# Cosine-similarity attention: the first pair split by head, ten K scales moved to VectorE, and instruction orders read from a table

## The chip, the cores and the metric

One core of a Trainium2 chip runs the whole kernel. A core has a matrix engine (TensorE, PE in the profile), three engines for elementwise work (VectorE or DVE, ScalarE or ACT, GpSimd or POOL), and SyncE (SP), which here only issues transfers between the chip's memory (HBM) and the core's memory (SBUF). PE writes to a second memory, PSUM, which is divided into banks. Each engine runs its own list of instructions in the order of the program and waits on semaphores for the others. The metric is the time of one execution in microseconds; the time before is the median of 8 runs, 197.62 us (196.11 to 199.24).

## The reference

```python
def reference(Q, K, V, tau):                       # each 8 x 12 x 512 x 64, float32; tau = 0.1
    Q_norm = Q / (np.linalg.norm(Q, axis=-1, keepdims=True) + 1e-10)
    K_norm = K / (np.linalg.norm(K, axis=-1, keepdims=True) + 1e-10)
    scores = np.einsum('bhqd,bhkd->bhqk', Q_norm, K_norm) / tau
    weights = np.exp(scores - np.max(scores, axis=-1, keepdims=True))
    weights = weights / (np.sum(weights, axis=-1, keepdims=True) + 1e-10)
    return np.einsum('bhqk,bhkd->bhqd', weights, V).astype(np.float32)
```

There are 96 heads of 512 queries and 512 keys with 64 numbers each. Every row of Q and K is divided by its length, so that a score lies between -10 and 10, and the maximum need not be subtracted.

## The kernel before

The kernel works on **48 pairs** of heads. For each pair these operations are made (the names are the keys in the code, and stand in the prediction as words):

- LD (L289) and LV (L292) load Q, K and V of the pair, 256 KB each, on SP. ST (L462) stores the result. Eighteen pairs of Q and K can lie in SBUF at once, and six of V.
- SQ squares Q and K. For most pairs this is one instruction on POOL over 1,024 numbers in each of 128 partitions (L310). For pairs 0, 1 and 2 the table `SQ_ON` gives Q and K separately to ACT, DVE or POOL (L303, L305).
- RED sums the squares of each row: on DVE directly (L335), or in two steps, SSQ on PE (L324), which adds eight groups of columns, and a shorter reduction on DVE (L331). One sum of every later pair, and both sums of pairs 1 to 3, go by PE.
- NEW makes one over the root of the sums. For pairs 0, 1 and 2 it is a logarithm and an exponential on ACT (LOG, L348, and L350) and a copy of Q's half to PSUM on DVE (L353). From pair 3 on it is made for two pairs at once, in eight short steps on DVE (L355 to L364).
- SCL multiplies with it and writes bf16 (L382): Q on DVE, **K on POOL** for all pairs. The list `K_ON_DVE`, which would send K to DVE, is empty.
- TR transposes on PE (L388, four instructions each for Q and K), and EVA copies the result from PSUM to SBUF: one copy on DVE (L405); for pair 0 K's half on ACT (L396) and Q's half on DVE (L400).
- SCO makes the scores on PE (L413). A pair has four chunks `c` of 128 keys, each for both heads. EXP takes the exponential of one chunk of both heads, 1,024 columns, on ACT (L424), straight from two PSUM banks. There are two such places, so the scores of chunk `c` wait for the exponential of chunk `c - 2`.
- VC converts V to bf16 on POOL (L429), with a column of ones beside it, so that PV, the product of the weights with V on PE (L438), also gives the sum of the weights. RCP (L453) and NRM (L455) on DVE divide by it.

Twelve matmuls on zeros (`warm`, L247) run on PE while the first loads are on their way.

**What sets the order.** Every operation is added to one list with a due time (`START`, `PERIOD` and the rest) and the operations that it needs. `schedule` plays them through with a table of durations, `TIMES`, and so fixes the order of each engine's instructions. Between due times 16.0 and 180.5 PE and ACT keep strictly to the order of the due times, as SP does throughout; DVE and POOL take what can start first among the next 60. `run` then writes each engine's list with the waits that are left. The order is thus fixed in the program; on the chip an engine stands at an instruction until its operands are there, whatever is ready behind it. SP loads in the order Q, K of pairs 0, 1, 2, then V of pair 0, and then Q, K and V in turn. POOL begins with the square of Q1, the K scales of pairs 0 and 1, V0, and the squares of pairs 3 and 4. ACT begins with the square of Q0, the square of K1, pair 0's logarithm, both squares of pair 2, and pairs 1's and 2's roots, all ahead of the first exponential.

Of the kernel before, what the change touches and what calls it, by code (L numbers as in the profile page):

```python
# [3 lines left out]
ALU = mybir.AluOpType  # L4
# [13 lines left out]
class Program:  # L18

    TIMES = {
        "exp": (0.903, 1.055), "exp1": (0.477, 0.63), "sqa": (0.48, 0.63), "sm_act": (0.12, 0.26),
        "cpa": (0.48, 0.63), "table": (1.3, 1.3),
        "sco": (0.322, 0.39), "pv": (0.127, 0.31), "tr": (0.223, 0.39), "warm": (4.4, 4.5),
        "eva": (0.597, 0.69), "eva1": (0.33, 0.42), "nrm": (0.34, 0.425), "rcp": (0.09, 0.178), "sclq": (0.593, 0.677),
        "red": (0.6, 0.685), "new": (0.11, 0.2), "sqv": (0.6, 0.69), "sm_dve": (0.1, 0.2),
        "sq": (1.85, 1.9), "sqp": (0.97, 1.02), "sclk": (1.0, 1.045), "vc": (0.585, 0.63), "sm_pool": (0.3, 0.35),
        "ld": (0.05, 2.1), "ssq": (0.245, 0.41), "redp": (0.131, 0.23),
    }  # L30
    WIRE = 0.72
    LATENCY = {"pe": 0.056, "act": 0.042, "dve": 0.038, "pool": 0.08, "sp": 0.08}
    SWITCH = 0.09
    START = {"sp": 0.8, "pool": 0.7, "dve": 0.7, "pe": 0.7, "act": 0.8}
    HEAD, TAIL = 16.0, 180.5
    FIXED = ("sp", "pe", "act")

# [10 lines left out]
    def schedule(self):  # L48
        engines = ("sp", "pool", "dve", "pe", "act")
        pending = {e: sorted((o for o in self.list if o.eng == e), key=lambda o: o.due) for e in engines}  # L50
        order = {e: [] for e in engines}
        free = dict(self.START)
        wire = 1.0
        tiled = False

        def ready_at(o):
            t = 0.0
            for n in o.needs:
                p = self.ops[n]
                if p.end is None:  # L60
                    return None
                if p.eng != o.eng or o.eng in ("dve", "pool") or o.own:
                    t = max(t, p.end + self.LATENCY[o.eng])
            return t

        left = len(self.list)
        while left:
            best = None
            for e in engines:
                pick = None  # L70
                wide = 1 if e == "sp" or e in self.FIXED and pending[e] and self.HEAD < pending[e][0].due < self.TAIL else 60
                for o in pending[e][:wide]:
                    r = ready_at(o)
                    if r is None:
                        continue
                    start = max(r, free[e])
                    if pick is None or start < pick[0] - 1e-9:
                        pick = (start, o)
                if pick is not None and (best is None or pick[0] < best[0]):
                    best = pick  # L80
            assert best is not None, [
                (e, [(o.key, [n for n in o.needs if self.ops[n].end is None]) for o in pending[e][:4]]) for e in engines]
            start, o = best
            e = o.eng
            pending[e].remove(o)
            order[e].append(o)
            left -= 1
            pitch, dur = self.TIMES[o.kind]
            if e == "pe":
                if o.kind == "sco" and not tiled:  # L90
                    start = max(start, free[e] + self.SWITCH)
                tiled = o.kind == "sco"
            o.start = start
            if o.slot is not None:
                wire = max(wire, start) + self.WIRE
                o.end = wire + dur
                free[e] = start + pitch
            else:
                o.end, free[e] = start + dur, start + pitch
        self.model_us = max(o.end for o in self.list)  # L100
        return order
# [67 lines left out]
def bass_cosine_similarity_attention_kernel(  # L169
# [71 lines left out]
    P.add("table", "act", "table", -1000, [], lambda e: e.preload_act_table_set("natural_log_exp_and_others"))  # L241
# [7 lines left out]

    P.add("wz", "dve", "sm_dve", -100, [], lambda e: e.memset(warm_in[:, :], 0.0))  # L250
# [28 lines left out]

    def pair(s):  # L280
# [6 lines left out]
        for w, x in ((0, Q), (1, K)):  # L287
            P.add(("LD", s, w), "sp", "ld", s, [key("SCL", s - R_QK, w), key("SQ", s - R_QK, 0)],
                  lambda e, w=w, x=x: e.dma_start(out=qk[iq][:, w], in_=src(x, s)),  # L289
                  slot=f"first{s}_{w}" if s in SQ_ON else f"qk{iq}")  # L290
# [5 lines left out]
        red = [key("RED", s - R_SQ, 0), key("RED", s - R_SQ, 1)]  # L296
        if s in SQ_ON:
            for w, eng in enumerate(SQ_ON[s]):
# [5 lines left out]
                else:  # L304
                    emit = lambda e, half=half, dst=dst: e.tensor_tensor(out=dst, in0=half, in1=half, op=ALU.mult)  # L305
                P.add(("SQ", s, w), eng, {"act": "sqa", "dve": "sqv", "pool": "sqp"}[eng],
                      due_sq(s) + 0.1 * w, [("LD", s, w), red[w]], emit)
        else:
            P.add(("SQ", s, 0), "pool", "sq", due_sq(s), [("LD", s, 0), ("LD", s, 1)] + red,
                  lambda e: e.tensor_tensor(out=sqf, in0=data, in1=data, op=ALU.mult))  # L310

        m = 8 * sizes[g]
# [3 lines left out]
        for w in range(2):  # L316
            sqs = ("SQ", s, w if s in SQ_ON else 0)
            dst = x2[:, w, c8 : c8 + 8]
            if (s, w) in session:
# [10 lines left out]
                P.add(("RED", s, w), "dve", "redp", due + 0.1, [("SSQ", s, w), key("NEW", g - R_X, 7)],  # L330
                      lambda e, bank=bank, dst=dst: e.tensor_reduce(  # L331
                          out=dst, in_=o_ps[bank][:, 320:384].rearrange("p (g e) -> p g e", e=8), axis=AX.X, op=ALU.add))
            else:
                P.add(("RED", s, w), "dve", "red", due_red(s) + 0.5 * w, [sqs, key("NEW", g - R_X, 7)],
# [5 lines left out]
        rq_g, rk_g = n_ps[:, g % R_X, 128 : 128 + m], xs[g][:, m : 2 * m] if acts else rk[g % R_X][:, 0:m]  # L340
        on_dve = [i for i in range(first[g], first[g] + sizes[g]) if i in K_ON_DVE]
        free = [[("SCL", i, k) for i in range(first[g - R_X], first[g - R_X] + sizes[g - R_X])] if g >= R_X else []
                for k in range(2)]
        reds = [("RED", i, w) for i in range(first[g], first[g] + sizes[g]) for w in range(2)]
        if s == first[g] and g in NORM_ON_ACT:
            at = NORM_ON_ACT[g]
            P.add(("LOG", g), "act", "sm_act", at, reds + ["eps"],
# [4 lines left out]
            P.add(("NEW", g, 6), "dve", "new", TF - 2.6, [("NEW", g, 7)],  # L352
                  lambda e: e.tensor_copy(out=rq_g, in_=xs[g][:, 0:m]))  # L353
# [22 lines left out]
        for w in range(2):  # L376
            dve = w == 0 or s in K_ON_DVE
            r = (tg[:, m + c8 : m + c8 + 8] if dve else rk_g[:, c8 : c8 + 8]) if w else rq_g[:, c8 : c8 + 8]
            r = r.rearrange("p (h t) -> p h t", h=2).unsqueeze(3).to_broadcast([128, 2, NT, DIM])
            P.add(("SCL", s, w), "dve" if dve else "pool", "sclq" if dve else "sclk", T0 - (2.85 if w and not dve else 2.55) - slack(s, M_SCL),  # L380
                  [("NEW", g, 6 + w + (dve and w)), key("TR", s - R_QN, w)],
# [4 lines left out]
            def tr(e, w=w):  # L386
                for t in range(NT):
                    last = e.transpose(  # L388
                        (t_k0 if s == 0 and w else t_ps[:, w])[:, t, :], qn[iqn][:, w, t].rearrange("p h d -> p (h d)"), ident[:, :])
                return last  # L390

            P.add(("TR", s, w), "pe", "tr", T0 - PERIOD + 0.9 * TR_AT[w],
                  [("SCL", s, w), key("EVA", s - 1) if not (s == 1 and w) else ("EVA", 0), "eye"], tr)
        if s == 0:
            P.add(("EVA", s, 1), "act", "cpa", -50, [("TR", s, 1)],
                  lambda e: e.activation(  # L396
                      out=qt[iqt][:, 1].rearrange("p t x -> p (t x)"),
                      in_=t_k0.rearrange("p t x -> p (t x)"), func=ACT.Copy))
            P.add(("EVA", s), "dve", "eva1", -50, [("TR", s, 0)],
                  lambda e: e.tensor_copy(  # L400
                      out=qt[iqt][:, 0].rearrange("p t x -> p (t x)"),
                      in_=t_ps[:, 0].rearrange("p t x -> p (t x)")))
        else:
            P.add(("EVA", s), "dve", "eva", T0 - 1.5, [("TR", s, 0), ("TR", s, 1), key("SCO", s - R_QT, NT - 1)],
                  lambda e: e.tensor_copy(  # L405
                      out=qt[iqt][:, :, :, :].rearrange("p w t x -> p (w t x)"),
                      in_=t_ps[:, :, :, :].rearrange("p w t x -> p (w t x)")))
        for c in range(NT):
            b = c % 2

            def sco(e, c=c, b=b):
                for h in range(2):
                    last = e.matmul(  # L413
                        out=sc_ps[:, 2 * b + h, :], lhsT=qt[iqt][64 * h : 64 * h + 64, 1, c, :],
                        rhs=qt[iqt][64 * h : 64 * h + 64, 0, :, :], start=True, stop=True)
                return last

            P.add(("SCO", s, c), "pe", "sco", T0 + 0.9 * c,
                  [("EVA", s), ("EVA", s, 1) if s == 0 else None, ("EXP", s, c - 2) if c >= 2 else key("EXP", s - 1, c + 2)], sco)
            for h in range(2) if last_pair and c == NT - 1 else (None,):  # L420
                hs = slice(0, 2) if h is None else slice(h, h + 1)
                P.add(("EXP", s, c) if h is None else ("EXP", s, c, h), "act", "exp" if h is None else "exp1", T0 + 0.9 * c + (h or 0) * 0.1,
                      [("SCO", s, c), key("PV", s - R_ET, 1, NT - 1)],
                      lambda e, c=c, b=b, hs=hs: e.activation(  # L424
# [54 lines left out]
WARM = 12  # L479
# [11 lines left out]
def slack(s, most):  # L491
    return most * min(1.0, s / 12)
# [33 lines left out]
```

## Time and profile before

| | |
|---|---|
| median of 8 runs | 197.62 us (196.11 to 199.24) |
| the profiled execution | 197.44 us, of which the span from its first to its last instruction is 195.5 us |
| ACT busy | 182.8 us, 93% of the span |
| PE busy | 177.6 us, 91% (the ends of matmuls are modelled) |
| DVE busy | 164.6 us, 84% |
| POOL busy | 162.8 us, 83% |
| first exponential starts | 11.16 us |
| the 193 exponentials | 177.4 us busy, 1,152 ns mean of one |
| mean granted PE clock | 0.991 |

A row of a timeline gives the start and the length in us, then the engine, the line of the kernel, the operation, what is written from what, the shapes, and how many instructions are merged (x). In brackets stands the idle time of the engine before it, and what ended the wait. Instructions of one engine overlap a little, so the time from one start to the next is shorter than the length of one. A row of the windows gives one stretch of time and how long each engine was busy in it.

### The profile page before, as it was taken

Reading aid. Unit: us, or ns where it says so; the run is one execution under the profiler, and the core shown is the slowest. Engines: PE = TensorE matmul, PEld = TensorE weight load, DVE = VectorE, ACT = ScalarE, POOL = GpSimd, SP = SyncE. Lnnn points to the kernel's source line nnn. Section 1 sums busy time; section 2 is a strip of 40 time slices with the busy share of each in tenths; the row PEclk is TensorE's granted clock in tenths of the full one; section 3 lists DMA queues with packets and bytes.
Section 4 is the critical chain, followed back from the end, with each engine's and each line's share of the span. In section 5 each row is a group of like instructions: output and inputs, shape, how many; then the busy total and the mean of one; then the engine's idle time right before and its main releaser. Section 6 shows DMA issues by size and latency. Waiting matters only on the chain.

```text
span 195.5 us, 6712 instructions
## 1 busy us (share of the span) xinstructions
PE 177.6 (91%) x2716; PEld 108.2 (55%) x2716; DVE 164.6 (84%) x573; ACT 182.8 (93%) x205; POOL 162.8 (83%) x150
## 2 busy tenths in 40 slices
PE   7469799599999999999999999999999999999983
PEld 2335466356565566566565566565565565555552
DVE  1657998779989999998988999989999988887744
ACT  3499799689999999999999999999999999999993
POOL 2599999999989999999999999999989996521200
PEclk9999999979999999999999999999999999999999
DMA  5999999997979889899989969989989965231133
GB/s 167 345 354 348 348 358 364 314 307 227 318 251 328 270 275 328 287 288 279 285 275 312 301 212 323 289 282 292 305 283 288 303 208 144 89 104 62 54 106 111
DMA packets 52270, 50.76 MB, mean 260 GB/s; under 512 B 3088, under 2 KB 52240, under 8 KB 52240
## 3 DMA queue, kind: packets, MB, share of 16 engines
q1 hardware_dynamic: 52240, 50.34, 80.6%
q8 instruction: 21, 0.34, 0.7%
q14 instruction: 9, 0.07, 0.1%
HBM read 37.75 MB, written 12.58 MB: 257 GB/s over the span
## 4 chain that ended last, share of the span: by engine, by line
ACT 76%; POOL 11%; DMA 3%; PE 3%; SPq 3%; DVE 1%; issue 1%
ACT et L424 76%; POOL sq L310 6%; DMA qk<-in_K_dram 3%; POOL qn L382 3%; SPq L289 2%; POOL vb L429 2%; PE scps L413 1%; PE ops L438 1%; PE tps L388 1%; SPq L292 0%; DVE ob L455 0%; DVE nps L335 0%; DVE qn L382 0%; PE ops L324 0%; DVE rd L453 0%
## 5 line engine op out<-in xcount | busy, mean ns | idle before, releaser
L424 ACT ACTIVATE et<-scps 128x1024 bf16<-128x1024 f32 (+1 forms) x193 | 177.4, 1152 | 3.7 <-PE scps L413 3.6
L310 POOL TENSOR_TENSOR sq<-qk 128x1024 bf16<-128x1024 f32 x45 | 85.8, 1906 | 0.7 <-DMA qk<-in_K_dram 0.6
L413 PE MATMUL scps<-qt 64*128 64x512 bf16 x384 | 75.2, 387 | 6.8 <-ACT et L424 1.8
L438 PEld LDWEIGHTS ops<-vb,et 128*128 128x128 bf16 x1536 | 57.5, 98 | 42.4 <-issue 29.9
L438 PE MATMUL ops<-vb,et 128*128 128x65 bf16 x1536 | 80.0, 196 | 0.2 <-ACT et L424 0.2
L382 POOL TENSOR_TENSOR qn<-qk,rk 128x512 bf16<-128x512 f32 x45 | 46.3, 1054 | 13.3 <-DVE rk L360 13.3
L388 PE MATMUL tps<-ident,qn 128*128 128x128 bf16 x380 | 37.1, 220 | 4.2 <-DVE qn L382 2.3
L455 DVE TENSOR_TENSOR ob<-ops,rd 128x256 f32<-128x256 f32 x96 | 40.4, 421 | 0.4
L405 DVE COPY qt<-tps 128x1024 bf16<-128x1024 bf16 x47 | 32.2, 685 | 4.0 <-PE tps L388 3.8
L413 PEld LDWEIGHTS scps<-qt 64*128 64x128 bf16 x384 | 19.4, 93 | 28.1 <-ACT et L424 16.2
L382 DVE TENSOR_TENSOR qn<-qk,nps 128x512 bf16<-128x512 f32 x48 | 32.2, 677 | 0.1
L335 DVE TENSOR_REDUCE nps<-sq 128x8 f32<-128x512 bf16 x44 | 29.9, 678 | 1.7 <-POOL sq L310 1.4
L429 POOL TENSOR_SCALAR vb<-vf 128x512 bf16<-128x512 f32 x48 | 30.5, 638 | 0.4 <-DMA vf<-in_V_dram 0.4
L453 DVE RECIPROCAL rd<-ops 128x4 f32<-128x4 f32 x96 | 17.2, 179 | 13.6 <-PE ops L324 7.9
L388 PEld LDWEIGHTS tps<-ident,qn 128*128 128x128 bf16 x380 | 22.6, 98 | 7.1 <-DVE qn L382 3.6
L324 PE MATMUL ops<-sq,ident 128*128 128x64 bf16 x400 | 19.7, 194 | 2.5 <-POOL sq L305 1.7
L324 PEld LDWEIGHTS ops<-sq,ident 128*128 128x128 bf16 x400 | 15.1, 98 | 3.2 <-POOL sq L305 2.2
L331 DVE TENSOR_REDUCE nps<-ops 128x8 f32<-128x64 f32 x46 | 9.4, 203 | 0.7 <-PE ops L324 0.7
L355 DVE TENSOR_TENSOR nps<-nps,ys 128x32 f32<-128x32 f32 (+1 forms) x46 | 8.8, 192 | 0.8
L356 DVE SCALAR_TENSOR_TENSOR nps<-nps,ys 128x32 f32<-128x32 f32 (+1 forms) x46 | 8.8, 192 | 0.6
L303 ACT ACTIVATE sq<-qk 128x512 bf16<-128x512 f32 x4 | 2.5, 626 | 4.0 <-DMA qk<-in_K_dram 2.5
L247 PE MATMUL ops<-warm_in,ident 128*128 128x512 bf16 x12 | 4.1, 513 | 1.4 <-POOL ident L237 1.4
(27 smaller groups left out, 31.7 us busy)
## 6 DMA issues: line engine op xcount, KB each, us to landing
qk<-in_Q_dram SPq DMA_DIRECT2D x48, 256.0 KB, 4.0
qk<-in_K_dram SPq DMA_DIRECT2D x48, 256.0 KB, 4.8
vf<-in_V_dram SPq DMA_DIRECT2D x48, 256.0 KB, 4.2
out_dram<-ob SPq DMA_DIRECT2D x47, 256.0 KB, 3.3
out_dram<-ob SPq DMA_DIRECT2D x2, 128.0 KB, 1.7
```

Source lines behind the costliest of these rows:

```text
L310: lambda e: e.tensor_tensor(out=sqf, in0=data, in1=data, op=ALU.mult))
L324: last = e.matmul(out=o_ps[bank][:, 320:384], lhsT=ident[:, :], rhs=sq[iqs][:, 8 * w : 8 * w + 8, 8 * k : 8 * k + 8], start=(k == 0), stop ...
L335: lambda e, w=w, dst=dst: e.tensor_reduce(out=dst, in_=sq[iqs][:, 8 * w : 8 * w + 8, :], axis=AX.X, op=ALU.add))
L382: lambda e, w=w, r=r: e.tensor_tensor(out=qn[iqn][:, w].rearrange("p t h d -> p h t d"), in0=qk[iq][:, w].rearrange("p h (t d) -> p h t d" ...
L388: last = e.transpose((t_k0 if s == 0 and w else t_ps[:, w])[:, t, :], qn[iqn][:, w, t].rearrange("p h d -> p (h d)"), ident[:, :])
L405: lambda e: e.tensor_copy(out=qt[iqt][:, :, :, :].rearrange("p w t x -> p (w t x)"), in_=t_ps[:, :, :, :].rearrange("p w t x -> p (w t x)")))
L413: last = e.matmul(out=sc_ps[:, 2 * b + h, :], lhsT=qt[iqt][64 * h : 64 * h + 64, 1, c, :], rhs=qt[iqt][64 * h : 64 * h + 64, 0, :, :], sta ...
L424: lambda e, c=c, b=b, hs=hs: e.activation(out=et[iet][:, c, hs, :], in_=sc_ps[:, 2 * b + hs.start : 2 * b + hs.stop, :], func=ACT.Exp, sca ...
L429: lambda e: e.tensor_scalar(out=vb[:, iq, :, :, 0:DIM].rearrange("p c h d -> p h c d"), in0=vf[iv][:, :, :].rearrange("p h (c d) -> p h c ...
L438: last = e.matmul(out=o_ps[h][:, 65 * t : 65 * t + 65], lhsT=et[iet][:, c, h, 128 * t : 128 * t + 128], rhs=vb[:, iq, c, h, :], start=(c = ...
L453: lambda e, h=h, grid=grid: e.reciprocal(out=rd[io][:, h, :], in_=grid[:, :, DIM]))
L455: lambda e, h=h, grid=grid: e.tensor_tensor(out=ob[io][:, h], in0=grid[:, :, 0:DIM], in1=rd[io][:, h, :].unsqueeze(2).to_broadcast([128, N ...
```

## The change

It has four parts.

1. **The first pair, head by head.** Q and K of pair 0 are loaded in four transfers of 128 KB, Q's by SP and K's by ACT, which issues them ahead of its table load. A new function, `head0`, makes square, reduction, root, scale, transpose and copy for each head alone: Q's squares on ACT, K's on POOL, the logarithm and two exponentials of each head on ACT, K's scale on POOL. Of the four copies three are on DVE, and that of K's second head is on ACT. The first two score chunks of pair 0, and their exponentials, are made head by head too, so there are 195 exponentials in all. The square of K of pair 2 goes from ACT to POOL.
2. **K on VectorE** for ten pairs: 1, 2, 3, 4, 9, 15, 21, 27, 33 and 39. For pairs 1 and 2 the copy of the root to PSUM takes K's half along; for the others one more step is added to NEW in its group (seven in all).
3. **Orders from a table.** `schedule` no longer plays anything through. It reads each engine's order from `ORDER`, as numbers in the list of operations; the waits are still worked out from what each operation needs. Some needs are written out more fully, because an order may now differ from the order of the due times.
4. **Dummy matmuls.** `warm` has 8 matmuls instead of 12. In PE's table an entry `-n` is a matmul of `n` columns on zeros into the first score bank: five between `warm` and the first transpose, and four more before the first scores.

```diff
+    def schedule(self):
+        order = {}
+        for e, text in ORDER.items():
+            order[e] = [self.list[int(x)] if x[0] != "-" else self.dummy(int(x[1:])) for x in text.split()]
...
+        return order
+
+    def dummy(self, columns):
+        return Op("dummy", "pe", "", 0, [], lambda e: self.fill(e, columns))
...
+    P.fill = lambda e, n: e.matmul(out=sc_ps[:, 0, 0:n], lhsT=ident[:, :], rhs=warm_in[:, 0:n], start=True, stop=True)
...
+    def head0(TF):
+        for h in range(2):
...
+            for w in range(2):
+                src_, dst = qk[0][:, w, h, :], sq[0][:, 8 * w + 4 * h : 8 * w + 4 * h + 4, :]
+                flat = dst.rearrange("p g d -> p (g d)")
+                if SQ0[w][h] == "act":
+                    emit = lambda e, a=src_, b=flat: e.activation(out=b, in_=a, func=ACT.Square)
+                else:
+                    emit = lambda e, a=src_, b=flat: e.tensor_tensor(out=b, in0=a, in1=a, op=ALU.mult)
...
+                P.add(("RED", 0, w, h), "dve", "redh", at + 0.2 + 0.1 * w, [("SQ", 0, w, h)],
...
+            P.add(("LOG", 0, h), "act", "ln", at + 0.4, [("RED", 0, 0, h), ("RED", 0, 1, h), "eps", "table"],
...
+                P.add(("NRMS", 0, w, h), "act", "sm_act", at + 0.5 + 0.01 * w, [("LOG", 0, h)],
...
+                P.add(("SCL", 0, w, h), "pool" if w else "dve", "sclph" if w else "sclh", at + 0.6 + 0.1 * w, [("NRMS", 0, w, h)],
...
+                P.add(("TR", 0, w, h), "pe", "tr", at + 0.8 + 0.1 * w,
+                      [("SCL", 0, w, i) for i in range(h + 1)] + [("EVA", 0, w, 0) if h else None, "eye"], tr)
+                eng = EVA0[w][h]
...
+            if s == 0:
+                for h in range(2):
+                    P.add(("LD", 0, w, h), "act" if w else "sp", "ldh", -1000 + h,  [],
+                          lambda e, w=w, x=x, h=h: e.dma_start(out=qk[iq][:, w, h], in_=src(x, s)[:, h]), slot=f"first{w}_{h}")
+                continue
...
-                  lambda e: e.tensor_copy(out=rq_g, in_=xs[g][:, 0:m]))
+                  lambda e: e.tensor_copy(out=n_ps[:, g % R_X, 128 : 128 + 2 * m], in_=xs[g][:, 0 : 2 * m]))
...
-            r = (tg[:, m + c8 : m + c8 + 8] if dve else rk_g[:, c8 : c8 + 8]) if w else rq_g[:, c8 : c8 + 8]
+            r = (rkd[:, c8 : c8 + 8] if dve else rk_g[:, c8 : c8 + 8]) if w else rq_g[:, c8 : c8 + 8]
...
+            for hs in ((0,), (1,)) if s == 0 and c < 2 else ((0, 1),):
...
-SQ_ON = {0: ("act", "dve"), 1: ("pool", "act"), 2: ("act", "act")}
+SQ_ON = {1: ("pool", "act"), 2: ("act", "pool")}
+SQ0 = (("act", "act"), ("pool", "pool"))
+EVA0 = (("dve", "dve"), ("dve", "act"))
...
-K_ON_DVE = ()
+K_ON_DVE = (1, 2, 3, 4, 9, 15, 21, 27, 33, 39)
...
-WARM = 12
-START, PERIOD = 8.3, 3.62
+WARM = 8
+START, PERIOD = 7.5, 3.62
...
+ORDER = {
+    "sp": (
+        "7 8 64 65 103 104 143 142 187 186 11 297 221 220 66 262 415 263 296 188 264 105 338 339 144 568 63 525 222 372 "
...
+    "pool": (
+        "0 1 2 4 14 27 22 67 35 107 145 189 50 223 89 265 206 282 128 299 172 341 237 248 271 375 358 418 313 452 347 "
...
+    "dve": (
+        "5 13 15 26 28 19 32 24 21 72 70 34 75 109 78 76 111 80 114 115 117 147 190 119 149 192 55 150 56 151 152 153 "
...
+    "pe": (
+        "6 -512 -256 -256 -256 -192 23 20 -256 -256 71 69 -128 33 36 108 -128 42 38 39 110 79 43 77 46 48 148 146 81 "
...
+    "act": (
+        "9 10 3 12 25 16 18 17 29 31 30 68 106 73 74 37 44 40 41 112 45 113 47 49 82 84 86 88 121 123 125 127 165 167 "
```

The numbers count the operations in the order in which they are added. Read back, the tables begin so (h0 and h1 are the heads of pair 0; Q1 is Q of pair 1):

- SP: Q0 h0, Q0 h1, Q1, K1, Q2, K2, K3, Q3, K4, Q4, V0, K7, K5, Q5, V1, Q6, Q10, K6, Q7, V4, V6, V2, Q8, K8, V3, K14, store 0, Q13, V5, Q9, K9, K10, V8.
- ACT: load K0 h0, load K0 h1, table load, square Q0 h0, square Q0 h1, root of h0 (K before Q), root of h1, square K1, square Q2, root of pair 1, copy of K0 h1, exponentials of chunk 1 h0, chunk 0 h0, chunk 0 h1, logarithm of pair 2, exponential of chunk 1 h1, root of pair 2, chunks 2 and 3, then the chunks of pair 1 and on.
- POOL: four small fills, square K0 h0, square K0 h1, scale K0 h0, square Q1, scale K0 h1, square K2, squares of pairs 3 and 4, V0, square 5, V1, square 6, V4, V6, V2, square 7, V3, square 8, K scale 5, V5, K scale 6, square 9, V8, square 10, K scale 7, square 11, K scale 8.
- DVE: four half reductions, scale Q0 h0, scale Q0 h1, copies K0 h0 and Q0 h0, reductions K1 and Q1, copy Q0 h1, root copy of pair 1, reduction Q2, scales K1 and Q1, reduction K2, copy of pair 1, root copy of pair 2, scales Q2 and K2, reductions Q3 and Q4, copy of pair 2.
- PE: warm, fills of 512, 256, 256, 256 and 192 columns, transposes K0 h0 and Q0 h0, two fills of 256, sums K1 and Q1, a fill of 128, transposes Q0 h1 and K0 h1, sum Q2, a fill of 128, scores of chunk 1 h0, chunk 0 h0, chunk 0 h1. Later, between the scores: transpose K5 ahead of the last chunk of pair 4, transpose K6 ahead of the second chunk of pair 5, transpose K7 ahead of the last chunk of pair 6.

## The prediction

> **What bounds the kernel now.** I read four views in this order: the windows of two stretches, the ScalarE (ACT) timeline, the head in the timeline, the costliest groups.
>
> ```profile
> 11.16:42.20 31.04, 25.97 (x382) 15.77 (x381) 25.05 (x87) 27.41 (x30) 30.93 (x26) 0.95 1.06 344
> 42.20:191.74 149.54, 143.99 (x2260) 88.41 (x2258) 133.30 (x471) 149.54 (x164) 126.61 (x113) 1.00 0.77 244
> ```
>
> Columns: stretch; length; busy us of PE, PE's weight loads, DVE, ACT, POOL; granted clock, DMA share, GB/s. From 42.20 to the last exponential ACT has no gap: 149.54 us for the exponentials there. In the timeline 30 of the 193 start before 42.20, so 163 stand here, 0.917 us each from start to start. Nothing done to other engines can shorten that stretch; it can only be disturbed. Before 42.20 ACT works 27.41 of 31.04 us: 3.6 us are missing, while POOL works 30.93, that is always.
>
> ```profile
> 11.16 11.20 ACT L424 ACTIVATE et<-scps 128x1024 bf16<-128x1024 f32 x12
> 23.40 12.12 ACT L424 ACTIVATE et<-scps 128x1024 bf16<-128x1024 f32 x13 [1.04 <-PE scps L413]
> 36.29 1.02 ACT L424 ACTIVATE et<-scps 128x1024 bf16<-128x1024 f32 x1 [0.78 <-PE scps L413]
> 38.20 1.02 ACT L424 ACTIVATE et<-scps 128x1024 bf16<-128x1024 f32 x1 [0.88 <-PE scps L413]
> 39.81 1.02 ACT L424 ACTIVATE et<-scps 128x1024 bf16<-128x1024 f32 x1 [0.59 <-PE scps L413]
> 41.12 5.76 ACT L424 ACTIVATE et<-scps 128x1024 bf16<-128x1024 f32 x6 [0.29 <-PE scps L413]
> ```
>
> Here the 3.6 us are five gaps (brackets: idle time, releaser). Counting exponentials, the first stands ahead of pair 3, the next three inside pair 6, the last ahead of pair 7. Inside pair 6 its own operands were there: PE runs in program order, and between pair 6's scores stand the transposes of pair 7, which wait for its scaled Q and K:
>
> ```profile
> 32.03 1.90 POOL L310 TENSOR_TENSOR sq<-qk 128x1024 bf16<-128x1024 f32 x1
> ...
> 33.97 0.69 DVE L335 TENSOR_REDUCE nps<-sq 128x8 f32<-128x512 bf16 x1
> ...
> 34.82 0.65 DVE L382 TENSOR_TENSOR qn<-qk,nps 128x512 bf16<-128x512 f32 x1
> ...
> 35.53 0.40 PE L388 MATMUL tps<-ident,qn 128*128 128x128 bf16 x4 [1.08 <-DVE qn L382]
> ...
> 36.33 2.05 POOL L382 TENSOR_TENSOR qn<-qk,rk 128x512 bf16<-128x512 f32 x2
> ...
> 37.44 0.40 PE L388 MATMUL tps<-ident,qn 128*128 128x128 bf16 x4 [0.96 <-POOL qn L382]
> ```
>
> POOL is late with squares and with the K scale of pair 7; DVE queues behind the first, PE behind both. So three things set the end: the start of the exponentials at 11.16, these gaps, and 193 x 0.917. The change touches the first two.
>
> **Head.** The path before:
>
> ```profile
> 6.74 0.63 ACT L303 ACTIVATE sq<-qk 128x512 bf16<-128x512 f32 x1 [2.49 <-DMA qk<-in_K_dram]
> ...
> 8.34 2.05 POOL L382 TENSOR_TENSOR qn<-qk,xs 128x512 bf16<-128x512 f32 x2 [1.20 <-ACT xs L350]
> ...
> 9.93 0.60 ACT L396 ACTIVATE qt<-scps 128x512 bf16<-128x512 bf16 x1 [0.84 <-PE scps L388]
> ```
>
> The sums of pair 0 are there at 6.29 (end of its second reduction), but ACT stands at the square of K1 until that load lands at 6.7, so the root (logarithm, exponential) comes at 7.28 to 8.3, K's scale to 9.4, transpose 9.5 to 9.9, copy to 10.53, scores 10.73, exponential 11.16; pair 1's first at 14.81.
>
> After, by durations of the same rows; a half costs the straight line through two sizes. POOL squares take 1.04 (512) and 1.90 (1024), so 0.61 for 256; ACT exponentials 0.80 and 1.15, so a 512 square of 0.63 falls to about 0.45; DVE's 0.685 falls to 0.42 (between 0.34, half of it, and 0.685).
> - First halves of Q and K, 262 KB together, landed by 3.6, as before's first load of that size. ACT issues two loads (0.45 each, as SP's) ahead of its 1.28 us table load: table done at 3.05, no loss.
> - Square on ACT to 4.05, on POOL to 4.2, reductions to 4.85, log and exponential (0.29, 0.20, with a 0.05 hand-over) to 5.5, K scale of head 0 on POOL to 6.1, transpose 6.55, copies of head 0 on DVE to 7.45. DVE's order puts the second Q scale before these copies.
> - Then the new bound. ACT's order puts the squares of K1 and Q2 and the root of pair 1 ahead of the copy of K head 1 and of every exponential. K1 lands at 6.7 as before: square to 7.35. Q2 by 7.4 (7.53 before is the latest): square to 8.0. Pair 1's reductions on DVE 8.2, log 8.5, exponential 8.75, copy 0.60, and the first half exponential at 9.2.
> - Four halves at 0.50 start to start (0.917 less the 0.36 to 0.43 that half the columns save), not two wholes: +0.2. Pair 2's root, formerly ahead of the exponentials, stands between them: +0.3. It waits for K2's square, now on POOL, and its reduction, queued behind two scales on DVE: 10.6, when ACT has just issued its third half. So pair 1's first comes at 13.4, not 14.81: **1.4 us gained**. Ends: 0.5 if Q2 or K2 lands 0.9 later (V0 etc. stand behind them, so hardly), 2.2 if each hand-over is as quick as the best.
>
> A rule speaks against this part. The Trainium skill, "DMA: Bandwidth & Descriptors", section "Issuing engines are not separate DMA queues": loads from two engines run on the same 16 DMA engines, so a second queue saves only issue time. The row: 123 GB/s at 2.0 to 2.5 us, 342 in the next half, so the engines are full from 2.5 us with one queue. By the rule K's first half gains the 0.48 us between SP's first two issues; by the row the byte count (262 KB moved by 3.05) decides. Either way pair 0's operands (7.45) wait for ACT at 8.7, so the sum stays 1.4. I take the row.
>
> **Dummies.** Eight warm-ups and five fills stand before the first transpose, the others between waits. Before, PE idles 1.69 us ahead of 7.19, and four transposes still take 0.39 us, two scores 0.39, with the clock at 1.00. So they gain 0; the harm is below 0.3 us, as a fill of 256 columns is half of a 512-column matmul (0.2 us once warm). "TensorE: Matmul & The Clock Gate", section "What's actually happening", puts the drop to half rate after an idle window of about 3.4 us. The trace differs: at 35 to 38 us PE was busy about half of each us, never idle that long, yet the clock was 0.50 from 39 to 41 and two scores took 0.61. By the rule no fill is needed at 5 to 8 us; by the row light use may suffice. If the clock did fall at the first scores, one transpose group and one score pair at half rate would cost 0.4 us.
>
> **K on VectorE.** POOL is relieved of ten scales at 1.02 start to start, and gets the K square of pair 2 (1.04) and K's square of pair 0, in time when it idled (2.0 to 6.1). DVE gets ten at 0.60 and seven norm steps at 0.17, loses one square and splits reductions. Pairs 1, 2, 3, 4 and 9 count for the gaps. I follow POOL's table (square 1.86, V copy 0.59, scale 1.01), loads landing every 0.75 us after K1 (262 KB at 350 GB/s), two squares of pair 0 done before: pairs 3 and 4 squared by 13.6, V0, 5, V1 by 16.6, then K6, the 18th load, due 17.2; square 6 to 19.1, V4, V6, V2 to 20.9, square 7, V3, square 8 to 25.2; K scale of 5 to 26.2, of 6 to 27.8, of 7 to 33.1, of 8 to 36. Before: 28.0, 31.5, 37.4, 38.4. Needed now, with exponentials 0.925 apart from 13.4: pair 5's K stands ahead of the last score of pair 4, whose exponential is due at 27.3; transposed at 26.6, score at 27.0, margin 0.3. Pair 6: margin 0.9. Pair 7 stands ahead of the score due at 34.7, margin 0.7.
>
> DVE is what is late next. From 16 to 28 us it was busy 11.16 of 12. Pairs 3 and 4 add there two scales and a norm step: 1.4 us against 0.84. In its fixed order reductions of squares stand ahead of copies, so the shortfall reaches ACT: I leave **0.6 us** of gaps (ends: 0, if work fits in the idle 2.25 us of 12 to 16; 3.6, if lateness only moves). Gain 3.0. After 42 us they cost nothing while DVE has room (16.2 us idle); the K scales of pairs 15 to 39 ask 0.77 each, once in six pairs of 3.67.
>
> **Table.** It adds no instruction; its worth is in the moves counted. SP issues V0 eleventh, not seventh: 0.5 us each, at 6 us, wanted at 13.6. The first store waits on SP behind 26 loads; nothing behind it is due soon.
>
> **Sum:** 197.44 (this run: span 195.5 and 1.94 around it) - 1.4 - 3.0 = 193.0. The median of runs lies 0.18 above this run, so **193.2**.
>
> **Rivals.**
> - Only the head counts: the fixed orders keep the gaps. For: before's PE and ACT orders were fixed too, and stalled. Against: the margins above. 197.6 - 1.4 = 196.2.
> - **Slower: loads fetched too early starve POOL.** SP's table brings K7, Q10, V4, V6 before V2, and POOL stands in order at each. At 0.75 us a load it holds with 0.3 to 0.7 us spare. A delay grows over the 27 loads after K1 that pairs 9 and 10 need: at 0.95 us (276 GB/s) it is 5.4, less 0.6 spare and the 5.0 that both gains bring at best, about even; at 1.05 (250) 8.1 - 0.6 - 5.0 = +2.5: 200.1. It decides from 0.95. For: 258 GB/s at 4.5 to 5.0 us. Against: 344 over 11 to 42.
> - Both gains are eaten by a DVE that trails (7.2 us of added work shown on ACT by 4 to 5): 197.6, no change.
> - All gaps go and the head gains 2.2: 191.8.
>
> **How the numbers follow.** About 0.5%, 1 us, is what a measurement here can tell from no change. Chances: forecast 0.60 (191.4 to 195.2), only head 0.12, slower 0.16, no change 0.07, still better 0.05. Faster 0.77, same 0.07, slower 0.16. The range 190.8 to 197.4 leaves out the slower case and little else.
>
> **What would show it.** First exponential near 9.2, pair 1's at 13.4; ACT gaps after that at 0.6 us instead of 3.6; POOL with gaps before 42 us; K scale of pair 7 before 34 us; clock 1.00 at 39 to 41. Wrong: loads landing slower than 0.85 us apart, POOL waiting for V loads, a DVE without gap after 42 us while ACT shows some.

## The result and the profile after

The changed kernel takes **194.79 us** (median of 11 runs, 193.43 to 195.94). Against the runs of the kernel before made beside it (median 197.44) the ratio is **0.987**, 95% interval 0.984 to 0.990: 2.6 us faster. (The ratios, here and below, leave out executions more than 1.5% slower than the fastest of their kernel; the medians do not.) The profiled execution took 195.31 us, with a span of 193.3.

Where the time went is read from the start of the exponentials, counted in the trace:

| | before | after | after less before |
|---|---|---|---|
| first exponential of pair 1 | 14.81 | 17.08 | **+2.26** |
| from there to pair 8's first | 30.11 | 25.55 | **-4.56** |
| from there to the last | 146.50 | 146.52 | +0.02 |

So the change has lost time in the head and won twice as much in the middle. The ScalarE timeline of the changed kernel:

```profile
4.00 0.42 ACT L227 ACTIVATE sq<-qk 128x256 bf16<-128x256 f32 x1 [0.20 <-DMA qk<-in_Q_dram]
7.81 0.30 ACT L236 ACTIVATE ys<-xs,eps 128x8 f32<-128x8 f32 x1 [3.39 <-DVE xs L233]
...
11.84 0.31 ACT L355 ACTIVATE ys<-xs,eps 128x16 f32<-128x16 f32 x1 [1.67 <-DVE xs L337]
...
13.04 1.57 ACT L445 ACTIVATE et<-scps 128x512 bf16<-128x512 f32 x3
...
15.27 174.69 ACT L445 ACTIVATE et<-scps 128x1024 bf16<-128x1024 f32 x191
```

The last row is the success: 191 exponentials with no gap that the timeline shows, where before had five ahead of 42 us. The windows say the same (columns as in the prediction): ACT is busy for all of 29.16 us, and POOL, which had no pause before, has 2 us of it. That pause is one wait, ahead of the K scale of pair 5, for its root from VectorE; the row of POOL's timeline stands below.

```profile
13.04:42.20 29.16, 27.27 (x429) 17.05 (x428) 27.96 (x99) 29.16 (x36) 27.18 (x25) 1.00 1.06 340
42.20:189.95 147.75, 139.65 (x2238) 88.50 (x2237) 134.60 (x478) 147.61 (x162) 121.00 (x106) 1.00 0.76 249
```

```profile
28.24 1.04 POOL L389 TENSOR_TENSOR qn<-qk,rk 128x512 bf16<-128x512 f32 x1 [1.95 <-DVE rk L367]
```

The second row of the ACT timeline is the failure: 3.39 us of waiting for a reduction of pair 0. Its cause is on POOL, in POOL's timeline:

```profile
1.33 0.74 POOL L180 MEMSET vb<- 128x144 bf16 x1
6.71 1.31 POOL L229 TENSOR_TENSOR sq<-qk 128x256 bf16<-128x256 f32 x2 [4.63 <-DMA qk<-in_Q_dram]
8.43 0.61 POOL L246 TENSOR_TENSOR qn<-qk,xs 128x256 bf16<-128x256 f32 x1 [0.41 <-ACT scps L240]
```

The two squares at 6.71 are those of **K**'s halves, and the releaser is a load of **Q**. That can't be right by the data. The program's own list of waits on POOL shows why:

```
L229 TensorTensor sq<-qk 128x256 [waits d_first1_0]
L229 TensorTensor sq<-qk 128x256 [waits d_first1_1]
L246 TensorTensor qn<-qk,xs 128x4x64 [waits s_act]
L308 TensorTensor sq<-qk 128x512
```

The change names the semaphore of a half load `first{w}_{h}`, and K's halves (w = 1) so get `first1_0` and `first1_1`. The whole loads of pair 1 are named `first{s}_{w}`: Q of pair 1 is `first1_0` and its K `first1_1`. The same names give the same semaphores. Each load adds 16 to its semaphore. SP's list is counted first, so Q1 gets the value 16 and K's first half 32, and the square of K's first half waits for both. In the trace that semaphore's 16th count is at 3.54 us, when K's half was there, and its 32nd at 6.63, when Q1 was; the square starts at 6.71. (The square of Q1, the last row, then needs no wait of its own.) The shared name is a hazard too. The square of K1 on ACT waits for 16 counts of `first1_1`, and K's second half alone brings them at 4.21 us, before K1 has landed (7.33). It comes out right only because it stands behind pair 0's roots on ACT, and these wait for the squares on POOL, which wait for all 32.

### The profile page after: what moved, and what is told of

Read it like the earlier page. It is cut to its first block, busy times and chain, and to the rows that moved or that the text cites. A ratio compares the mean times of both kernels' runs of the same rounds, so it can differ in the third digit from the quotient of the medians.

```text
span 193.3 us, 6756 instructions
## 1 busy us (share of the span) xinstructions
PE 175.6 (91%) x2729; PEld 110.6 (57%) x2729; DVE 168.4 (87%) x593; ACT 182.2 (94%) x211; POOL 155.4 (80%) x144
## 4 chain that ended last, share of the span: by engine, by line
ACT 84%; DMA 5%; PE 4%; POOL 2%; DVE 2%; issue 1%; SPq 1%; ACTq 0%; DVEq 0%; POOLq 0%
ACT et L445 83%; DMA qk<-in_Q_dram 3%; DMA out_dram<-ob 2%; PE ops L459 1%; PE scps L429 1%; POOL sq L313 1%; DVE ob L476 1%; POOL vb L450 1%; PE tps L395 0%; PE ops L330 0%; SPq L286 0%; DVE qt L402 0%; PE scps L256 0%; POOL qn L246 0%; POOL sq L229 0%
## 5 line engine op out<-in xcount | busy, mean ns | idle before, releaser
L313 POOL TENSOR_TENSOR sq<-qk 128x1024 bf16<-128x1024 f32 x45 | 84.8, 1898 | 0.4 <-DVE rd L474 0.4
L459 PE MATMUL ops<-vb,et 128*128 128x65 bf16 x1536 | 76.3, 194 | 0.7 <-POOL vb L450 0.2
L389 POOL TENSOR_TENSOR qn<-qk,rk 128x512 bf16<-128x512 f32 x37 | 38.2, 1045 | 18.1 <-DVE rk L367 17.9
L476 DVE TENSOR_TENSOR ob<-ops,rd 128x256 f32<-128x256 f32 x96 | 39.5, 417 | 1.0 <-DMA out_dram<-ob 0.4
L389 DVE TENSOR_TENSOR qn<-qk,nps 128x512 bf16<-128x512 f32 x57 | 37.8, 676 | 0.0
L395 PE MATMUL tps<-ident,qn 128*128 128x128 bf16 x376 | 34.2, 220 | 0.2
L450 POOL TENSOR_SCALAR vb<-vf 128x512 bf16<-128x512 f32 x48 | 29.6, 631 | 3.7 <-PE ops L459 1.9
L395 PEld LDWEIGHTS tps<-ident,qn 128*128 128x128 bf16 x376 | 21.6, 98 | 11.0 <-issue 4.7
L233 DVE TENSOR_REDUCE xs<-sq 128x4 f32<-128x256 bf16 x4 | 1.5, 418 | 5.8 <-POOL sq L229 3.1
L367 DVE SCALAR_TENSOR_TENSOR nps<-nps,ys 128x16 f32<-128x16 f32 (+1 forms) x30 | 5.1, 173 | 0.1
```

What stands on the lines that cost most here:

```text
L389: lambda e, w=w, r=r: e.tensor_tensor(out=qn[iqn][:, w].rearrange("p t h d -> p h t d"), in0=qk[iq][:, w].rearrange("p h (t d) -> p h t d" ...
L395: last = e.transpose(t_ps[:, w, t, :], qn[iqn][:, w, t].rearrange("p h d -> p (h d)"), ident[:, :])
L450: lambda e: e.tensor_scalar(out=vb[:, iq, :, :, 0:DIM].rearrange("p c h d -> p h c d"), in0=vf[iv][:, :, :].rearrange("p h (c d) -> p h c ...
L459: last = e.matmul(out=o_ps[h][:, 65 * t : 65 * t + 65], lhsT=et[iet][:, c, h, 128 * t : 128 * t + 128], rhs=vb[:, iq, c, h, :], start=(c = ...
L476: lambda e, h=h, grid=grid: e.tensor_tensor(out=ob[io][:, h], in0=grid[:, :, 0:DIM], in1=rd[io][:, h, :].unsqueeze(2).to_broadcast([128, N ...
```

## The experiments

Ratios are those to the kernel before, with 95% intervals. Each kernel ran 6 to 12 times.

| kernel | median us | ratio |
|---|---|---|
| changed kernel | 194.79 | 0.987 (0.984 to 0.990) |
| e1, own semaphores | 193.19 | 0.977 (0.973 to 0.981) |
| e2, e1 without dummies | 193.55 | 0.980 (0.975 to 0.985) |
| e3, e1 with one load queue | 193.65 | 0.978 (0.973 to 0.984) |
| e4, e1 with the scheduler's orders | 203.64 | 1.021 (1.014 to 1.029) |
| e5, e4 with K on POOL | 199.51 | 1.010 (1.004 to 1.016) |
| e6, before with K of eight pairs on VectorE | 201.17 | 1.018 (1.012 to 1.024) |
| e7, e1's table with K on POOL | 199.44 | 1.009 (1.005 to 1.014) |
| e8, e1 with exponentials first | 195.60 | 0.991 (0.987 to 0.995) |

**e1: the half loads get semaphores of their own.**

```diff
-slot=f"first{w}_{h}")
+slot=f"half{w}_{h}")
```

> The changed kernel, but the four half loads of pair 0 get semaphores of their own. In the changed kernel K's half loads carry the names first1_0 and first1_1, which are also the names of the whole loads of Q and K of pair 1, so the square of K's first half waits until both have counted, at 6.63 us, although its own 16 counts were there at 3.54. Theory A (the shared semaphore holds the head): POOL's first square starts near 3.6, the first exponential near 9.8 (then set by K1 at 7.3 and Q2 at 8.0), pair 1's first near 14.0 instead of 17.1, and the time falls by about 3 us to 191.5 to 192.5. Rival B (the first half of K is late because two queues share the DMA engines): POOL's first square stays near 6.7 and the time at 194.8. Rival C (the head is won but given back): first exponential near 9.8, but gaps of 2 us or more on ScalarE before 42 us, because POOL and the loads are no earlier; time 194 or more.

The first row is from POOL's timeline, the others from that of ScalarE:

```profile
3.61 1.28 POOL L229 TENSOR_TENSOR sq<-qk 128x256 bf16<-128x256 f32 x2 [1.53 <-DMA qk<-in_K_dram]
```

```profile
4.71 0.30 ACT L236 ACTIVATE ys<-xs,eps 128x8 f32<-128x8 f32 x1 [0.26 <-DVE xs L233]
...
7.82 1.38 ACT L306 ACTIVATE sq<-qk 128x512 bf16<-128x512 f32 x2 [1.85 <-DMA qk<-in_K_dram]
9.44 0.31 ACT L355 ACTIVATE ys<-xs,eps 128x16 f32<-128x16 f32 x1 [0.24 <-DVE xs L337]
...
10.64 1.57 ACT L445 ACTIVATE et<-scps 128x512 bf16<-128x512 f32 x3
```

The square starts at 3.61 and now names K's load. Pair 1's first exponential comes at 14.68 instead of 17.08, and the interval lies below that of the changed kernel. Rival B falls. Rival C falls too: pair 1 to pair 8 takes 25.55 us, as in the changed kernel, with two gaps of 0.4 us in all in the rest. But the head is slower than expected, with the first exponential at 10.64, and the time is 193.19, not 191.5 to 192.5. The wait of 1.85 us is for K1, which landed at 7.80, and Q2 landed at 8.55. Of all the kernels that ran this one-line edit has the lowest ratio; e2 and e3, which rest on it, can't be told from it.

**e2: no dummies.** All negative entries are left out of PE's table.

```diff
-        "6 -512 -256 -256 -256 -192 23 20 -256 -256 71 69 -128 33 36 108 -128 42 38
+        "6 23 20 71 69 33 36 108 42 38
```

> As e1, without the nine dummy matmuls in PE's table; the eight warm-ups stay. Theory of the prediction: the dummies gain nothing, so the time is that of e1 within 0.3 us. Rival: without them PE's clock falls to half in the wait ahead of the first transposes (as it did in the changed kernel at 9.1 us, where four transposes took 0.63 us); then transposes and scores of pair 0 take 0.6 instead of 0.4, and the first exponential and the time are 0.4 to 0.8 us later than e1.

PE's timeline:

```profile
4.37 0.63 PE L185 MATMUL ops<-warm_in,ident 128*128 128x512 bf16 x1
5.95 0.64 PE L256 MATMUL scps<-ident,qn 128*64 128x128 bf16 x4 [0.94 <-POOL qn L246]
...
15.95 1.00 PE L395 MATMUL tps<-ident,qn 128*128 128x128 bf16 x8
16.88 0.39 PE L429 MATMUL scps<-qt 64*128 64x512 bf16 x2
```

In this execution PE is slow from its last warm-up until 16 us: four transposes take 0.64 us where e1 takes 0.41. (The row of the granted clock shows 1.00 there, but the trace's record of that clock begins only at 16.8 us.) Pair 1's first exponential is at 16.06, 1.4 us behind e1. This execution is the slowest of e2's six (195.28 us; the others 192.96 to 194.23). The medians differ by 0.36 us and the intervals overlap, so neither expectation is settled. Nor is it shown that the missing dummies made PE slow: e4 and e5 have none either, and there PE was at its full rate by 5.8 and 5.9 us (last section).

**e3: one queue.** K's half loads are issued by SP, between those of Q.

```diff
-P.add(("LD", 0, w, h), "act" if w else "sp", "ldh", -1000 + h,  [],
+P.add(("LD", 0, w, h), "sp", "ldh", -1000 + h,  [],
```

The entries of the two loads move from ACT's table to SP's.

> As e1, but all four half loads are issued by SP in the order Q, K, Q, K, and none by ScalarE. If the second queue is worth something: K's first half lands about 0.45 us later, later loads shift by two issues of 0.45 us (K1 and Q2 about 0.9 later), first exponential 0.5 to 0.9 later, time 0.5 to 0.9 above e1. If only bytes count (loads are bound by the DMA engines and not by the issue): K1 and Q2 land as in e1 or earlier, the time within 0.3 us of e1.

Two rows of the ScalarE timeline, the squares of K1 and Q2:

```profile
6.47 0.63 ACT L306 ACTIVATE sq<-qk 128x512 bf16<-128x512 f32 x1 [0.21 <-DMA qk<-in_K_dram]
7.44 0.63 ACT L306 ACTIVATE sq<-qk 128x512 bf16<-128x512 f32 x1 [0.34 <-DMA qk<-in_Q_dram]
```

In its profile the later loads came earlier than in e1: K1 at 6.44 and Q2 at 7.42, against 7.80 and 8.55; pair 1's first exponential at 13.57. A gap of 0.52 us at 27.96 gives part of it back (pair 6: 32.62 against 32.87). The medians differ by 0.46 us, between the two expectations, and the intervals overlap. The second queue has no worth that could be measured.

**e4 and e5: the scheduler's orders.** e4 is e1 with `schedule`, `TIMES` and the constants of the kernel before put back (and estimates for the half operations); e5 also sets `K_ON_DVE = ()`.

> As e1, but the engine orders come from the scheduler of the kernel before, with its durations and estimates for the half operations, START 8.3; no dummies, as the table holds them. It keeps the head by halves, own semaphores and K of ten pairs on VectorE. If the table removes the gaps: the gaps before 42 us come back in part (1.5 to 3.6 us), time 193.5 to 195.5. If K on VectorE removes them: gaps under 1 us, time within 1 us of e1.

> As e4 (orders from the scheduler, head by halves, own semaphores), but K of all pairs except none is scaled on POOL, as in the kernel before. If K on VectorE is what removes the gaps: this is slower than e4 (203.6), by up to 4 us. If, without the table, K on VectorE does harm, because the scheduler lets VectorE trail and PE waits for its Q scales: this is faster than e4 by 2 to 6 us, 198 to 202.

The waits of e4 from 12 to 42 us (total, times, longest):

```profile
PEld tps L458 <- DVE qn L452: 5.9, 7, 1.7
ACT et L508 <- PE scps L492: 5.3, 9, 1.8
PE tps L458 <- DVE qn L452: 4.1, 4, 1.6
```

Transposes wait for VectorE's scales, and the exponentials for the scores behind them: 5.3 us of gaps. The expectation named 1.5 to 3.6 us of gaps and 193.5 to 195.5 us, and was too low in both. With K on POOL the same scheduler makes a kernel that is 1.1% faster by the ratios, as e5's second expectation has it; their intervals overlap a little, but every run of e5 is faster than the fastest of e4. How much of e4's loss is VectorE's lateness and how much PE's rate stays open: the mean granted clock was 0.948 to 0.974 in e4's executions and 0.974 to 1.00 in e5's. The scheduler has no dummies and guessed durations for the new operations, so it is not the best that a scheduler could make.

**e6: the kernel before, one part alone.**

```diff
-K_ON_DVE = ()
+K_ON_DVE = (3, 4, 9, 15, 21, 27, 33, 39)
```

> The kernel before with one edit: K of pairs 3, 4, 9, 15, 21, 27, 33 and 39 is scaled on VectorE (pairs 1 and 2 stay on POOL, as their root is not in PSUM there). K on VectorE removes the gaps by itself: ScalarE gaps fall from 3.6 to under 1.5 us, time 194.5 to 196. The table removes them: gaps stay at 2.5 us or more, time 196.5 or more.

The first expectation failed. The second holds in its numbers (196.5 or more), but neither named a loss: the part alone makes the kernel slower by 1.8%. The only profile is of the slowest execution (204.38 us; the others 199.95 to 201.47), so the cause is not read from it.

**e7: the table, with K on POOL.** Each of the ten scales moves from VectorE's list to POOL's.

```diff
-            dve = w == 0 or s in K_ON_DVE
+            dve = w == 0
```

> As e1 (193.2), with its table, but K of the ten pairs is scaled on POOL, each scale put into POOL's order at the place where POOL stood when VectorE made it in e1; the extra norm step stays. POOL gets ten times 1.05 us. The table alone removes the gaps: time within 0.7 us of e1. K on VectorE is needed: the gaps before 42 us come back, 2 to 4 us, time 195 to 197.

The ScalarE timeline:

```profile
17.20 1.02 ACT L445 ACTIVATE et<-scps 128x1024 bf16<-128x1024 f32 x1 [1.53 <-PE scps L429]
19.16 8.36 ACT L445 ACTIVATE et<-scps 128x1024 bf16<-128x1024 f32 x9 [0.94 <-PE scps L429]
27.98 24.86 ACT L445 ACTIVATE et<-scps 128x1024 bf16<-128x1024 f32 x27 [0.47 <-PE scps L429]
...
159.90 34.24 ACT L445 ACTIVATE et<-scps 128x1024 bf16<-128x1024 f32 x38 [0.61 <-PE scps L429]
```

The gaps are back, 2.9 us ahead of 42 us as the second expectation said, and six smaller ones after it, which it did not name; the time is 199.44, not 195 to 197. The table was not made for this placement, so e7 shows that this table needs K on VectorE, not what a table made for K on POOL could do.

**e8: exponentials first.** In e1 ScalarE waits 1.85 us for K1. Here two half exponentials of pair 0 are put there, and what they need is moved forward on POOL, VectorE and PE. ACT's part of the edit:

```diff
-        "9 10 3 12 25 16 18 17 29 31 30 68 106 73 74 37 44 40 41 112
+        "9 10 3 12 25 16 18 17 29 31 30 44 40 68 106 37 73 74 41 112
```

> As e1, with its table's beginning reordered: the second K scale of pair 0 ahead of the square of Q1 on POOL, pair 0's transposes and two scores ahead of the sums of pair 1 on PE, and two half exponentials ahead of the squares of K1 and Q2 on ScalarE, in the 1.85 us in which it waits for K1 in e1. Theory: the first exponential at 7.7 instead of 10.6, pair 1's first 0.7 to 1.0 earlier (13.8), time 192.2 to 192.8. Rival: the head is no longer what sets the end; POOL and the loads are, and what is won comes back as gaps: time 193.2 as e1.

The ScalarE timeline, and after it a row of PE's and one of the windows:

```profile
7.78 0.60 ACT L445 ACTIVATE et<-scps 128x512 bf16<-128x512 f32 x1 [1.59 <-PE scps L429]
8.65 0.60 ACT L445 ACTIVATE et<-scps 128x512 bf16<-128x512 f32 x1 [0.28 <-PE scps L429]
9.15 1.14 ACT L306 ACTIVATE sq<-qk 128x512 bf16<-128x512 f32 x2
...
10.93 0.31 ACT L355 ACTIVATE ys<-xs,eps 128x16 f32<-128x16 f32 x1
...
13.18 0.31 ACT L355 ACTIVATE ys<-xs,eps 128x16 f32<-128x16 f32 x1 [0.97 <-DVE xs L337]
```

```profile
12.47 0.61 PE L395 MATMUL tps<-ident,qn 128*128 128x128 bf16 x4 [0.55 <-DVE qn L389]
```

```profile
13.00:18.00 5.00, 5.00 (x38) 2.51 (x37) 3.31 (x9) 3.96 (x6) 4.71 (x4) 0.50 1.11 349
```

The first exponential came at 7.78 as expected, but pair 1's at 16.68, 2.0 us later than in e1. The squares of K1 and Q2, which pair 1 waits for, start at 9.15 instead of 7.82, behind the exponentials, and pair 1's logarithm comes at 10.93 instead of 9.44. That is 1.5 of the 2.0 us. Then PE, whose fills now all stand ahead of the sums of pair 1, is at the slow rate by 12.47 (four transposes 0.61, clock 0.50 until almost 19 us), and from pair 1 to pair 8 another 1.2 us is lost (26.73 against 25.55). The two causes came with one edit and were not run apart. An early exponential of pair 0 is worth nothing if pair 1's root is late.

## Why the prediction was right, and where it was not

The forecast of 193.2 and the range held the time, and the sign was right. The sum was right to 1.6 us because two errors cancelled in part, and that is luck. It is luck as well that e1, which does what the change was meant to do, takes 193.19, the forecast itself: its head gains 1.3 us less than forecast and its gaps 1.6 more.

- **Head: forecast 1.4 us gained, measured 2.3 lost.** The step that failed is "First halves of Q and K, 262 KB together, landed by 3.6" together with "Square on ACT to 4.05, on POOL to 4.2". The halves landed as said (3.36 and 3.54), but the square waited on a semaphore that Q1's load shares. The collision stands in the diff, in two slot names, and could have been read there. e1 takes it away and alone brings 2.4 us at pair 1.
- **A mis-sized term behind it.** "K1 lands at 6.7 as before" and "Q2 by 7.4" took one execution for the rule. In seven profiles with the second queue (the changed kernel and all runs but e3 and e6) Q2 landed between 7.8 and 8.6. In e1's execution the head with own semaphores is therefore worth 0.1 us (14.68 against 14.81), not 1.4. Where the two loads landed as forecast (e3: 6.44 and 7.42), pair 1's first exponential came at 13.57, against the 13.4 of the forecast. So the steps behind the loads were right, and the landing is the term that was mis-sized.
- **Gaps: forecast 3.0 gained, measured 4.6.** The 0.6 us left for a trailing VectorE did not come: it was busy 27.96 of 29.16 us and held POOL for 1.95 us ahead of the K scale of pair 5, but its delays reached no exponential. So all 3.6 us of idle time went. A gap costs more than its idle time: the exponential ahead of it lasts its full 1.02 to 1.09 us, not the 0.913 from start to start. Five gaps so cost 0.6 us more than their idle times add up to. The last 0.3 us lies in the other 23 steps (0.927 before, 0.913 after).
- **K on VectorE: right in direction, its cause too simple.** The K scale of pair 7 started at 35.20, not before 34 as forecast, and was still in time, as the exponentials were later too; in e1, with the head repaired, it starts at 33.24. But "After 42 us they cost nothing while DVE has room" said nothing of what they are worth there: e7 loses on that side too (pair 8 to the last: 149.9 us against 146.8 in e1).
- **Table: "It adds no instruction; its worth is in the moves counted"** is the weakest step. Four kernels, all with pair 0 by halves and own semaphores, show that neither part works alone. (The scheduler orders the head differently too: pair 1's first exponential is at 15.95 in e4 and 14.01 in e5, at 14.68 in e1 and 14.62 in e7.)

| orders | K on POOL | K of ten pairs on VectorE |
|---|---|---|
| scheduler | 1.010 (e5) | 1.021 (e4) |
| table | 1.009 (e7) | 0.977 (e1) |

  Moving K costs 1.1% under the scheduler and gains 3.2% under the table. The rival of a trailing VectorE is what the waits of e4 show without the table. The dummies are not what makes the table work: e2 has none and stands at 0.980. Which of the table's moves take the gaps away was not tried.
- **Dummies: "they gain 0"** is neither upheld nor refuted (e2). In the changed kernel they did not do their work, since POOL's late square left PE idle for 3.3 us and the clock was 0.50 from 9 to 11 us, with four transposes at 0.63.
- **Loads fetched too early** did not starve POOL: 340 GB/s from 13 to 42 us, and no V conversion with a wait ahead of it there. That rival's loss did not come.

## What to carry to other kernels

When loads are given semaphores by name, check that the names of new loads can't meet those of old ones: here the program still computes the same, by the luck of its order, and only an impossible releaser in the trace (K's square released by Q's load) gives it away. A part of a change and the order it was found with can be one thing, as here; undoing one of them may say nothing of what the other is worth alone. Gaps on the bounding engine are better read from start to start than from idle time.

## What the runs showed of the hardware

The time at which an early load lands varied from profile to profile by more than a microsecond: K1 landed between 6.44 and 7.83 us, Q2 between 7.42 and 8.57. A load is there when its 16th count is, and often the last count alone is late: in e1 15 counts of Q1 were there at 5.42 us and the last at 7.06. The kernels with two queues had Q2 at 7.8 to 8.6, those with one at 7.4, 7.5 and 8.0; three executions are too few to say that the queue does it.

When PE reaches its full rate varied too, and neither the warm-ups nor the fills settle it. These are the first transposes of pair 0 in e4 (eight warm-ups, no fills), in e3 and in e1 (eight warm-ups, five fills):

```profile
5.78 0.41 PE L319 MATMUL tps<-ident,qn 128*64 128x128 bf16 x4 [0.78 <-DVE qn L309]
```

```profile
6.16 0.64 PE L256 MATMUL scps<-ident,qn 128*64 128x128 bf16 x4
```

```profile
6.04 0.41 PE L256 MATMUL scps<-ident,qn 128*64 128x128 bf16 x4
```

With no fills four transposes took 0.41 us in e4 and 0.64 in e2 (at 5.95 us), with fills 0.41 in e1 and 0.64 in e3. The Trainium skill, "TensorE: Matmul & The Clock Gate", section "What's actually happening", asks for about 3.4 us of sustained work. The eight warm-ups run from 1.41 to 5.00 us in all four; that was enough in e4, and in e2 it was not.

The row of the granted clock does not show the start. It reads 1.00 from the first microsecond in every execution, but the trace's record of that clock has its first entry at 5.5 us in e4, 5.9 in e1, 7.2 in e3 and 16.8 in e2, each time with the full rate. Ahead of that entry 1.00 means that nothing is recorded, and the durations decide.
